# RWKV chunk products grouped by tile shape, and attention scores as 64-row products on both halves of the array

## The chip, the core and the metric

The kernel runs on one core of one Trainium2 chip. It is a single launch. The metric is device time in microseconds; lower is better. The core has a matrix engine (TensorE, PE in the profile, with its weight loads as PEld), a vector engine (VectorE, DVE), a scalar engine (ScalarE, ACT), GpSimd (POOL) and SyncE (SP), which issues all the transfers of this kernel from one queue. Products are written to PSUM, eight banks of 512 float32 columns on 128 partitions, and VectorE or ScalarE take them from there.

## What is computed

One step of a decoder layer for 512 prompt tokens and 8 x 4 sample tokens, 544 in all, with 1024 columns: a half-step feed-forward, a token-mixing sub-layer, a second half-step feed-forward, each with norms around it. The token mixing has two groups that work on the same projections: RWKV-7 with 8 heads of 64, and differential attention with 4 heads, each with two maps of 64 rows. Cut to what the change touches:

```python
def wkv_scan(r, w, k, v, kk, a, s0):
    def step(S, inp):
        r_t, w_t, k_t, v_t, kk_t, a_t = inp
        sa = jnp.einsum('bhvk,bhk->bhv', S, -kk_t)
        S = (S * w_t[:, :, None, :] + sa[..., None] * (kk_t * a_t)[:, :, None, :]
             + v_t[..., None] * k_t[:, :, None, :])
        return S, jnp.einsum('bhvk,bhk->bhv', S, r_t)
...
def diff_attend(q, k, v, q_pos, k_pos, table, lam):
    bias = rel_bias(q_pos, k_pos, table)
    s = jnp.einsum('bqhmd,bkhmd->bhmqk', q, k).astype(jnp.float32) * (A_QK_DIM ** -0.5)
    s = s + bias[None, :, None]
    s = jnp.where(k_pos[None, :] <= q_pos[:, None], s, NEG_INF)
    p = jax.nn.softmax(s, axis=-1)
    p = p[:, :, 0] - lam * p[:, :, 1]
    return jnp.einsum('bhqk,bkhd->bqhd', p.astype(v.dtype), v)
```

The kernel does the scan over the prompt in eight chunks of 64 tokens: within a chunk by products of its keys and queries, between chunks by a state of 64 x 64 for each head.

## The kernel before

**Layout.** Features lie on the partitions. Four tiles of 128 rows hold the eight RWKV heads, two to a tile: `b` counts the tiles, `e` the half (rows 0 to 63 or 64 to 127). An attention head is one tile of 128 rows, its two maps `m` again on the two halves. All products named here are float32, and the trace shows each such product as two records of weight load and of matmul. A product of 64 rows uses half the rows of the array, one with 64 output partitions half its columns; the profile writes the tile in front of the shape (`64*64 64x64` is a tile of 64 by 64 and a moving operand of 64 x 64).

**Stages.** Feed-forward (to about 420 us); projections of the RWKV columns with their preparation (to 584); inverses of the chunks' triangles on VectorE, beside the attention projections, with the first chunks in between (to 700); then attention over the prompt, the last chunks, the samples' RWKV chunk and the samples' attention over 32 pages of cache side by side (to about 823); output product; second feed-forward.

**A chunk.** `ahead(c)` does what needs only the chunk's own tokens: it loads `kbv` (keys, values) and `ar` (removal keys, queries) back from device memory, multiplies keys with both for each `b` and `e` (L755, tile 64 by 128, a bank for each `e`), masks them into `g` (L756), transposes (L759, L763) and forms the right-hand sides (L769). `chunk(c)` is the serial part: state against removal keys (L782), inverse (L788), next state (L795, tile 128 by 64), outputs: for each `b` and `e` state against queries (L806, tile 64 by 64) and behind it the chunk's own part (L807, tile 128 by 64), which adds to the same PSUM columns. Chunk 0 has no state product. Outputs are taken to `yr` by ScalarE (L808).

**Scores.** For each of 16 items (4 heads, 4 blocks of 128 queries, n = 128 to 512 keys) `scores` copies each map's 64 rows of the queries into its half of `qpad` (L904, ScalarE), whose other half is zero, and multiplies all 128 rows of it with all rows of the keys (L905). VectorE adds the bias and finds the maximum (L907), ScalarE exponentiates (L909). `weighted` transposes the result (L922) and multiplies it with the values (L927). Scores and `weighted` share three PSUM banks (`abank`); the last chunks' `ahead` has a single one (`xbank`).

**Order.** The order on each engine is not that of the source. The framework schedules all engines when the program is built, by its own times and by priorities (`advance` gives the serial part of a chunk high priority), and each engine then runs its list in that order. Transfers are issued by SP in the order of its list too, a transfer that must wait for a buffer holding back all behind it.

Of the kernel before, what the change touches and what calls it, by code (L numbers as in the profile page):

```python
# [9 lines left out]
FT = mybir.dt.float32  # L10
# [41 lines left out]
def build(ctx, tc, A):  # L52
# [38 lines left out]
    # matmuls ahead of the first data, so that the tensor engine's clock is up when it comes  # L91
# [15 lines left out]
    # ---------------------------------------------------------------- helpers  # L107
# [11 lines left out]
    def mm3(ps, w, x, first, last):  # L119
        """ps (+)= w.T @ x, each the exact sum of two float32r parts"""  # L120
        T.matmul(ps, w[0], x[0], start=first, stop=False)
        T.matmul(ps, w[0], x[1], start=False, stop=False)
        T.matmul(ps, w[1], x[0], start=False, stop=last)

    def dot(ps, w, xs, k0=0, ins=None):
        """ps = the sum over k of w[k].T @ xs[k], the parts of the weights that come last at the end"""
# [19 lines left out]
    def bank():  # L146
        return pw.tile([128, 512], FT, name="pb")
# [16 lines left out]
    def sums(pt, src, cols):  # L164
        """sums over the partitions that each of cols marks, of a half's tokens, which go on the partitions"""
# [4 lines left out]
    def sums4(ps, bank):  # L170
        """a half's sums, 32 rows (two times 16 alike) for each of four tiles, turned round: [token, tile, block, sum]"""
# [7 lines left out]
    def inv_sqrt(pt, n, scale=1.0, eps=None, least=None, y=None):  # L179
        """(scale * pt + eps) ** -0.5, or of at least `least`: a guess from the exponent, a step of  # L180
        the third order (two thirds of its result), a Newton step"""
# [23 lines left out]
    def spread(y, e, bank=bank):  # L205
        """tokens back to the free axis: each of a token's e values on its share of the partitions, in PSUM"""
# [30 lines left out]
    class Pre:  # L237
        """a block's input, gains applied; the rows' scale is left to whoever takes the product out"""
# [23 lines left out]
    def close_half(h, s, y, sq, gcol, pre=None, xp=None, spill=None, out=None):  # L262
        """the sub-layer's norm and residual, then the next one's input; in steps that other work goes between"""
# [44 lines left out]
    def opening(ws, xs, take):  # L308
        """the first products with a new input: half 1's side by side, as its rows get ready; taken out unscaled"""
# [14 lines left out]
    def products(wsrc, x, y, finish, per=1, wx=None, apart=False):  # L324
        """y[m] for all m and both halves, of weights that hold `per` m each; apart: half 1 after all of half 0"""
# [81 lines left out]
    # ---------------------------------------------------------------- first half-step  # L407
# [46 lines left out]
    # ---------------------------------------------------------------- token mixing  # L454
# [11 lines left out]
    # what lives from the projections to the output product  # L466
# [25 lines left out]
    def projected(i):  # L492
        """block i of the projected RWKV columns, behind the token before: what proj takes, what shifted reads"""
# [28 lines left out]
    def shifted(pr, dst, dsts):  # L522
        """mixed with the token before"""
# [55 lines left out]
    # negated biases over distances  # L579
# [10 lines left out]
    # a row for each partition, so that reading one place earlier on each gives a Toeplitz matrix  # L590
# [5 lines left out]
    for b in range(4):  # L596
# [14 lines left out]
        # decays: products over the chunk, of all tokens up to one and including it  # L611
# [6 lines left out]
        # removal keys, of unit length  # L618
# [11 lines left out]
        # keys and their share  # L630
# [45 lines left out]
    # unit triangular inverses: 32x32 blocks on one partition each, then one merge  # L676
# [25 lines left out]
    def merged():  # L702
        """the inverses' lower left blocks, in steps between the projections"""
# [27 lines left out]
    # queries, and in their place what they attend to  # L731
# [3 lines left out]
    # ---------------------------------------------------------------- RWKV, prompt: chunk after chunk  # L735
# [5 lines left out]
    def ahead(c, bank):  # L741
        """what a chunk needs from its own tokens alone"""
# [7 lines left out]
        kbt, vs = kv.rearrange("p (s b e k) -> p s b e k", s=2, b=4, e=2)[:, 0], kv.rearrange("p (s b e k) -> p s b e k", s=2, b=4, e=2)[:, 1]  # L750
        for e in range(2):
            rows = slice(e * HD, (e + 1) * HD)
            ps = bank()
            for b in range(4):
                T.matmul(ps[:, b * 128:(b + 1) * 128], kb[rows, b], ar[rows, b], start=True, stop=True)  # L755
            V.tensor_tensor(g[:, e], ps.rearrange("p (b t) -> p b t", t=128), gm, op=OP.mult)  # L756
# [8 lines left out]
        # right-hand sides: keys against values  # L765
# [9 lines left out]
    def chunk(c, state, ar, g, kbt, vs, rhs):  # L775
        # the state's part of the right-hand sides
# [14 lines left out]
        # next state  # L791
# [7 lines left out]
        # outputs  # L799
        ps = bank()  # L800
        for b in range(4):
            for e in range(2):
                rows = slice(e * HD, (e + 1) * HD)
                o = ps[rows, b * CH:(b + 1) * CH]
                if c:
                    T.matmul(o, state[rows, b], ar[rows, b, 1], start=True, stop=False)  # L806
                T.matmul(o, vs[:, b, e], g[:, e, b, CH:], start=not c, stop=True)  # L807
# [3 lines left out]
    # ---------------------------------------------------------------- attention projections  # L811
# [13 lines left out]
    def between(spot):  # L825
        """a step of the inverses' merging behind the products so far"""
# [44 lines left out]
    # ---------------------------------------------------------------- attention, prompt  # L871
    # lambda
# [11 lines left out]
    # negated biases: one Toeplitz tile for each head  # L884
# [7 lines left out]
    for t in qpads:  # L892
        G.memset(t, 0.0)
# [503 lines left out]
```

## Time and profile before

| | |
|---|---|
| median of 3 runs | 1316.78 us (1316.12, 1316.78, 1322.76) |
| span of the profiled execution | 1314.4 us |
| its time less the median | span 2.4 us below; no time beside the span is given for that execution |
| mean granted TensorE clock | 0.973 |
| PE busy | 1256.5 us (96%), 10354 matmul records |
| PEld busy | 1184.2 us (90%) |
| DVE / ACT / POOL busy | 696.4 / 461.2 / 503.1 us |
| L755, records and busy | 128, 16.6 us |
| L806 and L807, records and busy | 112, 18.4 us and 128, 19.4 us |
| L905, records in four widths, busy | 4 x 16, 2.5 + 5.0 + 5.9 + 7.5 us |

A record's duration is from its start to its modelled end, and records overlap, so mean durations do not add up to time on the path. What a group costs TensorE is read from the starts: that of its first record and that of the first record behind it. "Busy" of a group counts overlapping records once. The granted clock of a stretch is given beside its busy times, 1.00 for full speed.

### The profile page before, as it was taken

The page shows a single profiled execution, that of the slowest core. Times are in us where ns is not written, and L with a number is a line of the kernel's source. Part 1 is how long each engine was busy: PE and PEld are TensorE (multiplying, and loading weights), DVE is VectorE, ACT ScalarE, POOL GpSimd, SP SyncE. Part 2 cuts the span into 40 slices and gives each one's busy share as a digit, 9 for nine tenths or more (in the row PEclk, how much of TensorE's full clock was granted, in tenths as well). Part 3 has the DMA queues.
Part 4 walks back from the last instruction along what each step waited for, and adds up shares of the span by engine and source line. Part 5 has one row for each costly group of instructions (what it writes and reads, how often), then busy time and mean ns, then how long its engine had stood idle before and what let it go on. Part 6 is the DMA issues. An engine that isn't in the chain of part 4 may idle for free.

```text
span 1314.4 us, 25021 instructions
## 1 busy us (share of the span) xinstructions
PE 1256.5 (96%) x10354; PEld 1184.2 (90%) x10354; DVE 696.4 (53%) x1356; ACT 461.2 (35%) x878; POOL 503.1 (38%) x330
## 2 busy tenths in 40 slices
PE   8999999999998989989999999998899999999996
PEld 7999999999998888978887755888899999999995
DVE  7742034412448898879425367788842044412446
ACT  6433232312334444411114446555332233312331
POOL 2534433443346496633000022343534343433342
PEclk8999999999999999899899899999999999999998
DMA  5333223322232423353116357541323322322221
GB/s 198 99 95 97 81 81 97 95 83 81 85 109 87 150 87 124 135 180 110 59 50 190 129 177 262 182 131 47 113 81 97 94 79 86 97 85 79 82 61 68
DMA packets 54455, 142.06 MB, mean 108 GB/s; under 512 B 6050, under 2 KB 17058, under 8 KB 53191
## 3 DMA queue, kind: packets, MB, share of 16 engines
q1 hardware_dynamic: 54342, 140.48, 34.4%
q8 instruction: 81, 1.33, 0.4%
q14 instruction: 32, 0.25, 0.1%
HBM read 125.05 MB, written 16.72 MB: 108 GB/s over the span
## 4 chain that ended last, share of the span: by engine, by line
PE 45%; DVE 9%; ACT 1%; DMA 1%; issue 1%; SPq 0%; DVEq 0%; POOL 0%; ACTq 0%
PE mm L134 7%; PE mm L131 7%; PE mm L130 7%; PE pb L134 3%; PE pb L131 3%; PE pb L130 3%; DVE sqa L228 1%; PE pb L905 1%; DVE tmp L691 1%; PE pb L807 1%; PE pb L806 1%; PE pb L755 1%; DVE X L693 1%; PE pb L927 1%; PE mm L1099 1%
## 5 line engine op out<-in xcount | busy, mean ns | idle before, releaser
L116 POOL TENSOR_TENSOR wlo<-wraw,whi 128x1024 fp32r<-128x1024 f32 (+1 forms) x168 | 399.9, 2384 | 540.7 <-ACT whi L114 488.3
L130 PE MATMUL mm<-xh,whi 128*128 128x272 f32 x1160 | 303.1, 292 | 9.1 <-DVE q_f L820 3.5
L131 PE MATMUL mm<-xl,whi 128*128 128x272 f32 x1160 | 303.5, 293 | 4.7 <-DVE xl L248 4.7
L114 ACT ACTIVATE whi<-wraw 128x1024 fp32r<-128x1024 f32 (+1 forms) x176 | 182.6, 1039 | 253.8 <-PE mm L131 152.0
L130 PEld LDWEIGHTS mm<-xh,whi 128*128 128x128 f32 x1160 | 221.6, 191 | 11.3 <-DVE q_f L820 4.1
L131 PEld LDWEIGHTS mm<-xl,whi 128*128 128x128 f32 x1160 | 221.7, 191 | 6.6 <-DVE xl L248 6.3
L134 PE MATMUL mm<-xh,wlo 128*128 128x272 f32 x1160 | 179.4, 298 | 0.0
L134 PEld LDWEIGHTS mm<-xh,wlo 128*128 128x128 f32 x1160 | 162.8, 197 | 0.3
L130 PE MATMUL pb<-xh,whi 128*128 128x272 f32 x568 | 150.5, 295 | 1.6 <-ACT ga L371 0.9
L131 PE MATMUL pb<-xl,whi 128*128 128x272 f32 x568 | 149.2, 294 | 0.0
L358 DVE TENSOR_TENSOR up<-up,ga 128x272 f32<-128x272 f32 x88 | 111.7, 1271 | 8.2
L130 PEld LDWEIGHTS pb<-xh,whi 128*128 128x128 f32 x568 | 110.3, 194 | 2.8 <-ACT ga L371 1.1
L131 PEld LDWEIGHTS pb<-xl,whi 128*128 128x128 f32 x568 | 109.9, 194 | 0.3 <-issue 0.2
L387 DVE TENSOR_TENSOR up<-mm,rpre 128x272 f32<-128x272 f32 x54 | 23.8, 442 | 114.9 <-PE mm L134 114.8
L134 PE MATMUL pb<-xh,wlo 128*128 128x272 f32 x568 | 83.2, 288 | 0.0
L134 PEld LDWEIGHTS pb<-xh,wlo 128*128 128x128 f32 x568 | 75.6, 188 | 0.0
L357 ACT ACTIVATE ga<-ga 128x272 f32<-128x272 f32 x88 | 38.0, 432 | 71.5 <-DVE ga L386 63.4
L386 DVE TENSOR_TENSOR ga<-mm,rpre 128x272 f32<-128x272 f32 x53 | 23.2, 438 | 73.7 <-PE mm L134 73.7
L130 PE MATMUL mm<-hd0h,whi 128*128 128x272 f32 x242 | 62.0, 289 | 0.0
L131 PE MATMUL mm<-hd0l,whi 128*128 128x272 f32 x242 | 61.9, 288 | 0.0
L130 PE MATMUL mm<-hd1h,whi 128*128 128x272 f32 x220 | 56.4, 289 | 0.0
L131 PE MATMUL mm<-hd1l,whi 128*128 128x272 f32 x220 | 56.3, 288 | 0.0
(406 smaller groups left out, 2277.5 us busy)
## 6 DMA issues: line engine op xcount, KB each, us to landing
wraw<-in_ff_in_dram SPq DMA_DIRECT2D x87, 512.0 KB, 3.6
wraw<-in_ff_out_dram SPq DMA_DIRECT2D x32, 512.0 KB, 3.6
wraw<-in_w_in_dram SPq DMA_DIRECT2D x26, 512.0 KB, 3.9
pg<-in_cache_k_dram SPq DMA_DIRECT2D x32, 256.0 KB, 3.7
pg<-in_cache_v_dram SPq DMA_DIRECT2D x32, 256.0 KB, 5.1
wraw<-in_w_out_dram SPq DMA_DIRECT2D x16, 512.0 KB, 4.1
wraw<-in_ff_out_dram SPq DMA_DIRECT2D x16, 384.0 KB, 3.2
cat_d<-cat SPq DMA_DIRECT2D x4, 1280.0 KB, 5.0
```

Source lines behind the costliest of these rows:

```text
L114: S.activation(hi, raw, AF.Copy)
L116: eng.tensor_tensor(lo, raw, hi.bitcast(FT), op=OP.subtract)
L130: T.matmul(ps, hi, xs[k][0], start=k == 0, stop=False)
L131: T.matmul(ps, hi, xs[k][1], start=False, stop=False)
L134: latest[0] = T.matmul(ps, wcols(w, k0 + k)[1], xs[k][0], start=False, stop=k == n - 1).ins
L228: eng.tensor_tensor(self.acc, self.acc, sq, op=OP.add)
L357: S.activation(g, g, AF.Silu)
L358: V.tensor_tensor(u, u, g, op=OP.mult)
L386: V.tensor_tensor(g, pg, pre.rs[s], op=OP.mult)
L387: V.tensor_tensor(u, pu, pre.rs[s], op=OP.mult)
L691: V.tensor_tensor(tv, lb[:, j + 1:, j:j + 1].to_broadcast([128, n, m]), X[:, j:j + 1, :m].to_broadcast([128, n, m]), op=OP.mult)
L693: V.tensor_tensor(X[:, j + 1:, :m], X[:, j + 1:, :m], tv, op=OP.subtract)
```

## The change

Three edits; everything else is the same but for comments and docstrings, which are taken out, so that lines move by a few.

1. In `ahead`, both banks of L755 are taken first, and the products go `b` by `b`, with `e` as the inner loop; masking follows for both.
2. In `chunk`, the eight state products of the outputs come first, then the eight of the chunk's own part. As two halves of one bank are now open over four `b` at once, the first matmul of each half (`b == 0`) starts the accumulation and the last one ends it.
3. In `scores`, both maps' products come first, each of 64 rows of queries and keys, straight from `q_f` and `k_f`, on the half where they lie. `qpad`, its memsets and the copies of L904 go. Here the work on TensorE is named L898 after the change, the transposes L916, the product with the values L921; the outputs' own part is L808.

```diff
@@ ahead
-        for e in range(2):
-            rows = slice(e * HD, (e + 1) * HD)
-            ps = bank()
-            for b in range(4):
-                T.matmul(ps[:, b * 128:(b + 1) * 128], kb[rows, b], ar[rows, b], start=True, stop=True)
-            V.tensor_tensor(g[:, e], ps.rearrange("p (b t) -> p b t", t=128), gm, op=OP.mult)
+        pair = [bank() for _ in range(2)]
+        for b in range(4):
+            for e in range(2):
+                rows = slice(e * HD, (e + 1) * HD)
+                T.matmul(pair[e][:, b * 128:(b + 1) * 128], kb[rows, b], ar[rows, b], start=True, stop=True)
+        for e in range(2):
+            V.tensor_tensor(g[:, e], pair[e].rearrange("p (b t) -> p b t", t=128), gm, op=OP.mult)
@@ chunk
-        for b in range(4):
-            for e in range(2):
+        outs = [(b, e, ps[e * HD:(e + 1) * HD, b * CH:(b + 1) * CH]) for b in range(4) for e in range(2)]
+        if c:
+            for b, e, o in outs:
                 rows = slice(e * HD, (e + 1) * HD)
-                o = ps[rows, b * CH:(b + 1) * CH]
-                if c:
-                    T.matmul(o, state[rows, b], ar[rows, b, 1], start=True, stop=False)
-                T.matmul(o, vs[:, b, e], g[:, e, b, CH:], start=not c, stop=True)
+                T.matmul(o, state[rows, b], ar[rows, b, 1], start=b == 0, stop=False)
+        for b, e, o in outs:
+            T.matmul(o, vs[:, b, e], g[:, e, b, CH:], start=not c, stop=not c or b == 3)
@@ scores
-    # a head's two queries, each with zeros for the other's rows
-    qpads = [ap_.tile([128, 2, 128], FT, name=f"qpad{j}", bufs=1) for j in range(2)]
-    for t in qpads:
-        G.memset(t, 0.0)
...
-        qpads.append(qpads.pop(0))
-        qpad = qpads[-1]
...
+        both = [abank() for _ in range(2)]
         for m in range(2):
             rows = slice(m * 64, (m + 1) * 64)
-            ps = abank()
-            S.activation(qpad[rows, m], q_f[rows, i, qb * 128:(qb + 1) * 128], AF.Copy)
-            T.matmul(ps[:, :n], qpad[:, m], k_f[:, i, :n], start=True, stop=True)
+            T.matmul(both[m][:, :n], q_f[rows, i, qb * 128:(qb + 1) * 128], k_f[rows, i, :n], start=True, stop=True)
+        for m, ps in enumerate(both):
```

What the scheduler makes of it, at three places. On TensorE, around the outputs of one chunk (`set` holds `g` and the values, `x8` is eight instructions in a row), before:

```order
L795 MATMUL pb<-set 64x64
L905 MATMUL pb<-k_f,qpad_7710 128x256
L795 MATMUL pb<-set 64x64 x7
L806 MATMUL pb<-ar,state 64x64
L807 MATMUL pb<-set 64x64
...
L905 MATMUL pb<-k_f,qpad_7711 128x256 x2
```

and in the changed kernel:

```order
L898 MATMUL pb<-k_f,q_f 128x256
L796 MATMUL pb<-set 64x64 x8
L806 MATMUL pb<-ar,state 64x64 x8
L808 MATMUL pb<-set 64x64 x8
L898 MATMUL pb<-k_f,q_f 128x256 x3
```

The alternation of L806 and L807 is now two groups of eight, in every chunk from 1 to 7. The score products stand in pairs, of which two of the sixteen are separated by other work (the first of them here).

On TensorE, L755 of chunk 0, of chunk 3 and of the last chunk (the number of `pb` tells the bank, and so the half), in the changed kernel:

```order
L755 MATMUL pb_6434<-ar_6430,kbv_6428 128x128
L755 MATMUL pb_6435<-ar_6430,kbv_6428 128x128
L755 MATMUL pb_6434<-ar_6430,kbv_6428 128x128
...
L755 MATMUL pb_7288<-ar_7284,kbv_7282 128x128 x4
...
L755 MATMUL pb_7289<-ar_7284,kbv_7282 128x128 x4
...
L755 MATMUL pb_8351<-ar_8347,kbv_8345 128x128 x2
```

Chunk 0 alternates between the halves, and so does chunk 4 with other work in between; chunk 1 has three, three, one, one; chunks 2, 3, 5, 6 and 7 have all four of one half and then the other, as all had before. The two products of the last chunk now stand right behind the state product of chunk 6:

```order
L783 MATMUL pb<-state,ar 64x64 x8
L755 MATMUL pb<-ar,kbv 128x128 x2
L962 MATMUL mm<-cst,sx 128x128 x4
```

where before they came 32 rows of the order behind it, beyond the first page products. On SP, the transfers that they need, before:

```order
L1059 DMA tb_7888<-in_table_dram 32x4 x4
...
L1087 DMA pg_8238<-in_cache_k_dram 128x512
L744 DMA kbv<-cat_d 128x4x192
L746 DMA ar<-cat_d 128x4x128
```

and in the changed kernel (`pg` are pages of the cache, the `...` stands for sixteen of them):

```order
L1053 DMA tb_7878<-in_table_dram 32x4 x4
L746 DMA ar<-cat_d 128x4x128
...
L1081 DMA pg_8222<-in_cache_k_dram 128x512
L744 DMA kbv<-cat_d 128x4x192
```

`ar` of the last chunk moved ahead of the sixteen page loads, `kbv` stays behind them.

## The prediction

> **What bounds the kernel now.** I read the first part of the page, then the busy times in stretches of 20 us or so, then the order of time on TensorE. In the rows of stretches the first two columns are the stretch and its length, then the busy time of PE, PEld, DVE, ACT and POOL, the granted clock, the DMA share and GB/s.
>
> ```profile
> PE 1256.5 (96%) x10354; PEld 1184.2 (90%) x10354; DVE 696.4 (53%) x1356; ACT 461.2 (35%) x878; POOL 503.1 (38%) x330
> ...
> 700.00:720.00 20.00, 20.00 (x270) 15.26 (x268) 11.09 (x39) 11.57 (x32) 0.00 (x0) 1.00 0.77 218
> 760.00:780.00 20.00, 20.00 (x152) 9.40 (x151) 10.50 (x28) 7.69 (x24) 5.17 (x5) 1.00 0.63 185
> 780.00:800.00 20.00, 20.00 (x172) 11.87 (x171) 13.72 (x49) 11.63 (x33) 3.40 (x3) 1.00 0.88 304
> 800.00:825.00 25.00, 23.74 (x147) 13.35 (x146) 20.12 (x54) 15.96 (x36) 8.54 (x6) 1.00 0.67 226
> ```
>
> The change touches only what runs from 584 to 823 us. There TensorE is busy without a break up to 812 us, while VectorE and ScalarE have a third to a half of their time free. So what TensorE saves there comes off the end, until another engine is reached. Two waits say the same from the other side: VectorE and ScalarE stand waiting for exactly the products that the change edits (columns: total us, times, longest).
>
> ```profile
> DVE sc L907 <- PE pb L905: 15.5, 12, 4.1
> ...
> ACT yr L808 <- PE pb L807: 42.1, 8, 7.5
> ```
>
> **The outputs of a chunk.** Each product is two records. These are the first and the last rows of one chunk's output products, in order of time (start, length, what, tile, shape, records), and then two neighbours that stand in groups of one shape.
>
> ```profile
> 709.39 0.33 PE L806 MATMUL pb<-ar,state 64*64 64x64 f32 x2
> 709.64 0.33 PE L807 MATMUL pb<-set 128*64 128x64 f32 x2
> ...
> 713.24 0.33 PE L807 MATMUL pb<-set 128*64 128x64 f32 x2
> 713.50 1.13 PE L905 MATMUL pb<-k_f,qpad 128*128 128x256 f32 x4
> ...
> 715.68 0.68 PE L782 MATMUL pb<-state,ar 64*64 64x64 f32 x16
> 716.29 0.70 PE L905 MATMUL pb<-k_f,qpad 128*128 128x256 f32 x2
> ...
> 768.04 0.69 PE L795 MATMUL pb<-set 128*64 128x64 f32 x16
> 768.65 0.32 PE L806 MATMUL pb<-ar,state 64*64 64x64 f32 x2
> ```
>
> Start to start, the sixteen products take 713.50 - 709.39 = 4.11 us, 0.257 each. Eight products of the shape of L806 in one group take 716.29 - 715.68 = 0.61 us (L782, which also goes from half to half), and eight of the shape of L807 take 768.65 - 768.04 = 0.61 us (L795). Grouped, a chunk's outputs cost 1.22 us, and 2.89 us go. The order of the change shows the two groups whole in all seven chunks that have both kinds (chunk 0 has no state product): 7 x 2.89 = **20.2 us**. Whether the cost came from the change of shape, or from L807 adding onto the columns that L806 has only just written, does not matter here: both are removed.
>
> The Trainium skill, TensorEngine Tiling (Array Packing), section Restrictions and Gotchas, speaks against part of this: row tiles may not write one PSUM bank at the same time, and both halves' state products do go to one bank. By it the eight of L806 would run one after the other, some 0.4 us longer in each chunk, and the saving would be about 17 us, as an estimate from that section. L782 has the same layout and takes 0.61 us for eight, so the row decides.
>
> **The products of a chunk's own tokens (L755).** Eight products of 64 rows by 128 columns, four on one half and then four on the other.
>
> ```profile
> 584.46 1.68 PE L755 MATMUL pb<-ar,kbv 64*128 64x128 f32 x16 [0.34 <-DMA ar<-cat_d]
> 586.07 0.66 PE L759 MATMUL pb<-cst,kbv 128*128 128x128 f32 x4
> ```
>
> 1.61 us for eight, 0.20 each. Run in pairs they would save 0.8 us a chunk, 6.4 us in all. But the order built from the change alternates fully only for chunks 0 and 4 (there cut by other work) and in part for chunk 1; for the other five it still has one half after the other. Two to four pairs in each of three chunks, less the pair at the turn that already overlaps before: 1.1 us. Neighbours of another shape rise from 28 to 32; at 0.15 us a switch (the 0.257 of an output less the 0.10 that its 64 columns take at the rate of L755's 128) that costs 0.6. Net **0.5 us**.
>
> **The scores.** A pair of score products (both maps) now has 64 rows each, on the two halves. The row of the line with its four shapes (durations in ns, first and last start, shapes), and two pairs with the row behind each:
>
> ```profile
> L905 PE MATMUL pb<-k_f,qpad x64: 275/484/595, 705.6 to 812.3; 128*128 128x256 f32 x16, 128*128 128x128 f32 x16, 128*128 128x384 f32 x16, 128*128 128x512 f32 x16
> ...
> 781.48 1.46 PE L905 MATMUL pb<-k_f,qpad 128*128 128x384 f32 x4
> 782.86 0.68 PE L1182 MATMUL pb<-gsq,cst 128*32 128x272 f32 x2
> ...
> 788.95 1.88 PE L905 MATMUL pb<-k_f,qpad 128*128 128x512 f32 x4
> 790.77 1.91 PE L1099 MATMUL mm<-pg,qz 128*32 128x256 f32 x26
> ```
>
> Sixteen records of a shape are four pairs. A pair of 384 columns takes 1.38 us, one of 512 takes 1.82, so 128 columns of a pair cost 0.44 us and all sixteen pairs 4 x (1+2+3+4) x 0.43 = 17.1 us. That a product on each half runs at the same time is shown here only for tiles of 64 by 64 on the diagonal:
>
> ```profile
> 783.47 1.07 PE L1034 MATMUL mm<-vx,kvt 64*64 64x512 f32 x4
> 784.47 0.66 PE L1145 MATMUL mm<-cst,ov 128*128 128x128 f32 x4
> ```
>
> Two products of 512 columns in 1.00 us, where one alone of that width costs 0.85 (half of a pair above). For 64 by 128, where both halves write all 128 partitions, in two banks, no row shows it. Bounds: full overlap halves 17.1 and, with the two pairs that the order separates, saves 7.5; no overlap saves nothing. I take full overlap, since L1034 is the nearest row. Against it stand switches: neighbours of another shape go from 21 to 33, 12 x 0.10 to 0.15 = 1.2 to 1.8 us. Net **6.0 us** (from -1.8 to 6.3). The ScalarE copies of the queries go too, off the path: they cost ScalarE alone,
>
> ```profile
> L904 ACT ACTIVATE qpad<-q_f x32: 293/307/312, 690.6 to 797.9; 64x128 f32<-64x128 f32 x32
> ```
>
> 32 x 0.3 = 9.6 us where it is half idle. I cost them at nothing.
>
> **What is late next.** TensorE saves 20.2 + 0.5 + 6.0 = 26.7 us of work. Two things catch it. First the end of the stage, where the chain of waits already passes through VectorE (start, length, what):
>
> ```profile
> 812.95 0.69 DVE sc L907
> 813.99 0.92 DVE orp L1194
> 814.91 0.57 issue
> 815.48 0.50 DVE yr L1189
> ```
>
> VectorE is 80% busy from 800 us on, and 69% from 780. The scores that run behind 776 us (two pairs of 384 columns, four of 512) save 2 x 0.64 + 4 x 0.85 = 4.7 us, and most of that will be waited for: 3.5 (0 to 4.7). Second the keys of the last chunk. SP issues in its order:
>
> ```profile
> 696.08 18.03 SPq L1087 DMA_DIRECT2D pg<-in_cache_k_dram  x16
> 714.21 0.39 SPq L744 DMA_DIRECT2D kbv<-cat_d  x1
> ...
> L744 SPq DMA_DIRECT2D kbv<-cat_d x8: 359/374/497, 580.0 to 714.2; - x8
> DMA to landing us min/median/max: 3.3/3.5/4.9
> ...
> 730.11 1.12 PE L782 MATMUL pb<-state,ar 64*64 64x64 f32 x16
> 739.19 0.49 PE L755 MATMUL pb<-ar,kbv 64*128 64x128 f32 x2
> ```
>
> The load of kbv stays behind sixteen page loads, 18 us of issuing, and lands at 718 to 719 us. Before, L755 needs it at 739. In the changed order the first two of these products stand right behind the state product of chunk 6, which was at 730 (L782), and TensorE comes there five chunk outputs (14.5 us) and four score pairs of 256 columns (1.7 us) earlier: at 714. If SP's stream starts as early as before, everything on TensorE waits 5 us there; if it moves up with the projections that release it (two outputs stand ahead of them, 5.8 us), the load lands at 713 and nothing waits. I take 1.5 (0 to 5), and 1 for waits that I cannot name (0 to 3). Together **6 us given back** (0 to 13).
>
> **The clock.** Twice the clock falls just behind such output products (at 680 to 684 and 722 to 726 us):
>
> ```profile
> 680.00:684.00 4.00, 4.00 (x38) 2.96 (x34) 0.85 (x2) 0.00 (x0) 0.00 (x0) 1.00 0.00 0
> 684.00:688.00 4.00, 4.00 (x23) 3.65 (x23) 0.44 (x1) 0.38 (x1) 0.00 (x0) 0.57 0.25 69
> ...
> 724.00:728.00 4.00, 4.00 (x25) 3.12 (x24) 0.47 (x1) 0.77 (x2) 0.00 (x0) 0.68 0.00 0
> 728.00:732.00 4.00, 4.00 (x36) 2.35 (x35) 0.42 (x1) 1.31 (x8) 0.00 (x0) 0.50 0.01 4
> ```
>
> Lost: 4 x (0.43 + 0.32 + 0.50) = 5.0 us. If the alternation starved the array, both go; a new wait can bring one back (3.3). I take **2 us** gained (5.0 gained to 3.3 lost).
>
> **Sum.** -20.2 - 0.5 - 6.0 + 6 - 2 = -22.7 us against the span of 1314.4: 1291.7. The median of the runs shown is 1316.8, 2.4 above that span, so 1294.1.
>
> **Rivals.**
> 1. The halves of 64 by 128 do not overlap. For it: no row of such a pair. Against: L1034. The scores then only pay their switches (1.8) and L755 its 0.6; -20.2 + 2.4 + 4 (fewer waits) - 2 = -15.8, which gives 1301.
> 2. The gain is caught by waits: VectorE at the end and kbv in the middle at their full 13 us, with no gain of clock: -26.7 + 13 = -13.7, 1303; with a lost spell of clock as well, 1306. For it: the 80% of VectorE and the SP order. Against: SP's first load in that stream waits for TensorE, so it moves up too.
> 3. The full gain, waits near 1 and both spells of clock gone: -26.7 + 1 - 5 = -30.7, 1286.
> 4. Slower: arrays filled by halves and short waits keep the clock down in the whole stage from 640 to 800 us. From 45 us at half clock on, the 22.7 us are eaten; 60 us would give 1294 + 30 = 1324. For it: spells of 0.50 to 0.57 with TensorE busy by its records. Against: they follow the alternation that goes, and groups of halves (L782, L795) stand in stretches at 1.00. The Trainium skill, TensorE: Matmul & The Clock Gate, section Part 1: The HAM clock gate, tells of micro-idles between groups that make the gate oscillate; here only the two spells above look like it.
>
> That the change doesn't do what it says holds for L755, and stands in the sum.
>
> **Chances.** Forecast (1288 to 1299) 0.58; rival 1 0.14; rival 2 0.11; rival 3 0.12; rival 4 0.05. The range 1285 to 1306 takes in the forecast, rival 1, and most of 2 and 3, some 0.85. A measurement here tells about 0.5% (6.6 us) from nothing, so faster means below 1310.2: 0.92; within 0.5%: 0.04 (rival 2 at its worst); slower: 0.04.
>
> **What would show it.** Outputs: L806 and the line behind it in groups of 16 records, 0.61 us each. L755: alternate halves 0.1 us apart only in chunks 0, 1 and 4. Scores: a pair of 512 columns in 0.9 to 1.0 us rather than 1.82. Waits: TensorE idle for kbv or VectorE, 5 to 7 us between 640 and 810 us. Clock: 1.00 behind the outputs. Wrong if the outputs stay near 4 us, or if TensorE idles more than 13 us in that stage.

## The result and the profile after

The changed kernel takes 1289.65 us (median of four runs, 1288.69 to 1290.02), the kernel before on the same chip 1318.97 (median of four): ratio 0.9775, 95% interval 0.9753 to 0.9796. The profiled execution spans 1286.9 us where that of before spans 1314.4. The prediction was 1294 us (1285 to 1306) and faster. Intervals here and below leave out runs more than 1.5% above the fastest of their kernel; that left out three of the ten runs of the scores alone, at 1343 to 1346 us.

The page's first line of the changed kernel, and its rows by stretches (start and end of the stretch, its length, then the busy time of PE, PEld, DVE, ACT and POOL, the granted clock, the DMA share and GB/s):

```profile
PE 1225.1 (95%) x10354; PEld 1160.3 (90%) x10354; DVE 694.2 (54%) x1356; ACT 450.4 (35%) x846; POOL 501.9 (39%) x328
```

```profile
580.00:632.00 52.00, 45.27 (x468) 43.13 (x469) 48.70 (x91) 9.92 (x13) 18.37 (x8) 0.94 0.45 139
632.00:799.30 167.30, 162.78 (x1934) 115.64 (x1934) 91.85 (x278) 68.51 (x190) 18.88 (x19) 0.99 0.51 168
799.30:891.20 91.90, 85.83 (x649) 81.45 (x646) 80.77 (x164) 50.28 (x105) 35.09 (x23) 0.98 0.40 128
```

The second of these stretches ends with the first product of the output projection, the third with the first product of the last half-step. The same pieces of work of the kernel before, where these two products stand at 823.0 and 918.6 us:

```profile
580.00:632.00 52.00, 46.19 (x472) 44.15 (x472) 48.55 (x90) 9.75 (x12) 16.95 (x7) 0.95 0.45 136
632.00:823.00 191.00, 189.74 (x1931) 136.44 (x1925) 93.09 (x277) 78.67 (x219) 20.12 (x22) 0.96 0.47 148
823.00:918.60 95.60, 88.32 (x656) 82.46 (x653) 79.46 (x165) 51.29 (x109) 37.44 (x23) 0.98 0.38 122
```

This is the whole balance. The pieces are 338.6 us before and 311.2 after: 27.4 of the 27.5 us come from them. TensorE's busy time in them falls by 324.3 - 293.9 = 30.4 us, its idle time rises from 14.3 to 17.3, by 3.0. So almost all of TensorE's saving reached the end. (The prediction has TensorE busy without a break from 584 to 812 us. The rows show 5.8 us of idle time from 580 to 632 us, and 6.7 after the change; from 640 to 812 us the kernel before has none.)

The outputs of the chunk that the prediction showed at 709 us, now (start, length, line, tile, shape, records):

```profile
697.72 0.68 PE L806 MATMUL pb<-ar,state 64*64 64x64 f32 x16
698.34 0.69 PE L808 MATMUL pb<-set 128*64 128x64 f32 x16
698.95 0.91 PE L898 MATMUL pb<-k_f,q_f 64*128 64x256 f32 x5
```

698.95 - 697.72 = 1.23 us where it was 4.11. All seven chunks show 1.23. A pair of scores of 512 columns, and one of 384, each with the row behind it:

```profile
785.21 1.13 PE L898 MATMUL pb<-k_f,q_f 64*128 64x512 f32 x4
786.27 0.55 PE L214 MATMUL pb<-cst,rx 128*128 128x128 f32 x3
...
736.55 0.92 PE L898 MATMUL pb<-k_f,q_f 64*128 64x384 f32 x4
737.39 0.41 PE L1120 MATMUL mm<-cmb,ssc 128*32 128x128 f32 x2
```

1.06 us for 1.82, and 0.84 for 1.38: products of 64 by 128 on the two halves do overlap. Chunk 0's products of its own tokens alternate, and take 585.46 - 584.36 = 1.10 us for 1.61:

```profile
584.36 1.16 PE L755 MATMUL pb<-ar,kbv 64*128 64x128 f32 x16 [0.27 <-DMA ar<-cat_d]
585.46 0.66 PE L760 MATMUL pb<-cst,kbv 128*128 128x128 f32 x4
```

The new waits of TensorE are these (in brackets the idle time and what ended it):

```profile
711.99 0.68 PE L755 MATMUL pb<-ar,kbv 64*128 64x128 f32 x4 [1.01 <-DMA kbv<-cat_d]
...
789.50 0.55 PE L214 MATMUL pb<-cst,rx 128*128 128x128 f32 x3 [1.08 <-DVE yr L1183]
790.67 0.65 PE L1199 MATMUL mm<-fsq,ones 128*32 128x272 f32 x2 [0.62 <-ACT fsq L1198]
...
794.88 0.68 PE L1176 MATMUL pb<-gsq,cst 128*32 128x272 f32 x2 [1.12 <-ACT gsq L1175]
```

And the clock, in the stretches where the kernel before had 0.57, 0.68 and 0.50:

```profile
684.00:688.00 4.00, 4.00 (x76) 3.41 (x75) 2.43 (x12) 0.68 (x2) 0.00 (x0) 1.00 0.70 214
724.00:728.00 4.00, 4.00 (x74) 2.62 (x74) 2.74 (x12) 1.87 (x7) 0.00 (x0) 1.00 0.39 122
728.00:732.00 4.00, 3.78 (x43) 3.00 (x41) 2.74 (x16) 3.01 (x10) 0.00 (x0) 1.00 0.91 292
```

### The profile page after: what moved, and what is told of

It reads as the page before. It is cut to its first block, busy times and chain, and to the rows that moved or that the text cites. A ratio compares the mean times of both kernels' runs of the same rounds, so it can differ in the third digit from the quotient of the medians.

```text
span 1286.9 us, 24967 instructions
## 1 busy us (share of the span) xinstructions
PE 1225.1 (95%) x10354; PEld 1160.3 (90%) x10354; DVE 694.2 (54%) x1356; ACT 450.4 (35%) x846; POOL 501.9 (39%) x328
## 4 chain that ended last, share of the span: by engine, by line
PE 75%; DVE 18%; DMA 2%; ACT 2%; issue 2%; POOL 0%; SPq 0%; DVEq 0%; ACTq 0%
PE mm L134 14%; PE mm L131 14%; PE mm L130 14%; PE pb L131 7%; PE pb L130 7%; PE pb L134 7%; DVE sqa L228 2%; DVE xl L248 2%; DVE tmp L691 2%; DVE pn L276 1%; PE pb L755 1%; DVE X L693 1%; PE mm L1093 1%; PE pb L898 1%; PE pb L168 1%
## 5 line engine op out<-in xcount | busy, mean ns | idle before, releaser
L130 PE MATMUL mm<-xh,whi 128*128 128x272 f32 x1160 | 304.2, 293 | 10.2 <-DVE ga L386 2.7
L134 PE MATMUL mm<-xh,wlo 128*128 128x272 f32 x1160 | 176.3, 295 | 0.0
L358 DVE TENSOR_TENSOR up<-up,ga 128x272 f32<-128x272 f32 x88 | 114.9, 1308 | 8.2
L228 DVE TENSOR_TENSOR sqa<-sqa,sq 128x272 f32<-128x272 f32 x73 | 56.1, 776 | 17.6 <-ACT sq L227 16.4
```

The costliest lines, as they stand in the source:

```text
L130: T.matmul(ps, hi, xs[k][0], start=k == 0, stop=False)
L134: latest[0] = T.matmul(ps, wcols(w, k0 + k)[1], xs[k][0], start=False, stop=k == n - 1).ins
L228: eng.tensor_tensor(self.acc, self.acc, sq, op=OP.add)
L358: V.tensor_tensor(u, u, g, op=OP.mult)
```

## The experiments

### One edit at a time

Three kernels, each the kernel before with one of the three edits.

```diff
 e1: the outputs in two groups (each edit abridged)
+for b, e, o in outs:
+    T.matmul(o, state[rows, b], ar[rows, b, 1], start=b == 0, stop=False)
+for b, e, o in outs:
+    T.matmul(o, vs[:, b, e], g[:, e, b, CH:], start=not c, stop=not c or b == 3)
 e2: scores of 64 rows
-T.matmul(ps[:, :n], qpad[:, m], k_f[:, i, :n], start=True, stop=True)
+T.matmul(both[m][:, :n], q_f[rows, i, qb * 128:(qb + 1) * 128], k_f[rows, i, :n], start=True, stop=True)
 e3: L755 half by half in turn, into two banks
+pair = [bank() for _ in range(2)]
+for b in range(4):
+    for e in range(2):
+        T.matmul(pair[e][:, b * 128:(b + 1) * 128], kb[rows, b], ar[rows, b], start=True, stop=True)
```

> Kernel before with the second edit alone: a chunk's state outputs in one group, then its own-part outputs in one group; L755 and the scores stay as before. Theory (the gain is the alternation of shapes in the outputs, and the two half-clock spells belong to it): 7 x 2.89 = 20.2 us of TensorE work go, both spells between 680 and 732 us go (5 us, of which some 0.5 lies inside the outputs' own figure), 1 to 2 us come back as waits, so 22 to 25 us less than before, ratio 0.981 to 0.983. Rival a (the spells come from the scores or from L755): -18 to -20 us with a granted clock of 0.5 to 0.7 still in two stretches of 4 us between 640 and 800 us. Rival b (the outputs' gain was caught by waits and the scores made the rest): under 15 us.

> Kernel before with the third edit alone: score products of 64 rows on both halves, no padded queries. Theory: a pair of 512 columns goes from 1.82 to 1.06 us as in the changed kernel, all pairs save 6 us, 1 to 3 of them are waited for at the end of the stage where VectorE is 80% busy, so 3 to 6 us less than before; the outputs stay at 4.1 us a chunk and at least one half-clock spell stays. Rival (the scores hide waits that the outputs would otherwise meet, or the spells go with the padded queries): 8 us or more less, with clock 1.00 from 640 to 800 us.

> Kernel before with the first edit alone: the products of a chunk's own tokens written half by half in turn into two banks. Theory: only chunks 0 and 4 and part of 1 come out alternating, net 0.5 us, so within 2 us of before. Rival (the order of the other work changes with it, through the two banks that are taken at once): 2 to 6 us either way.

Measured against 1319.6 us of the kernel before on that chip (its runs from 1315.4 to 1327.2): the outputs alone 1296.5 us, ratio 0.981 (0.977 to 0.985), as expected. The scores alone are not faster but **slower**, 1328.6 us, ratio 1.010 (1.006 to 1.015), and the pairs alone too, 1334.7 us, 1.012 (1.007 to 1.016). By these ratios the first part saves 25 us and the other two lose 13 and 15 (by the medians 23, 9 and 15); together the three save 29. That was in no expectation.

The outputs alone show the two groups in all seven chunks, 705.45 - 704.23 = 1.22 us here, beside the old scores:

```profile
704.23 0.68 PE L805 MATMUL pb<-ar,state 64*64 64x64 f32 x16
704.84 0.69 PE L807 MATMUL pb<-set 128*64 128x64 f32 x16
705.45 1.13 PE L905 MATMUL pb<-k_f,qpad 128*128 128x256 f32 x4
```

No half clock stands behind them. There is a new spell of it, though, from 645 to 652 us, before the first of these groups; it comes up again at the end.

In the trace of the scores alone their line did what it should, 13.36 us for 19.16. L755 in the pairs alone did not: it takes 17.58 us for 15.60, with 24 of its 128 records at half clock. What grew is, first of all, time at half clock. These are stretches of the pairs-only kernel, cut where its clock changes:

```profile
681.57:684.98 3.41, 3.41 (x27) 2.54 (x27) 0.08 (x1) 0.11 (x1) 0.00 (x0) 1.00 0.00 0
684.98:688.39 3.41, 3.41 (x17) 3.16 (x18) 0.00 (x0) 0.28 (x1) 0.00 (x0) 0.50 0.33 82
695.22:698.63 3.41, 3.41 (x28) 2.53 (x28) 1.52 (x9) 0.00 (x0) 0.00 (x0) 1.00 0.65 221
698.63:708.87 10.24, 10.24 (x67) 8.25 (x67) 3.09 (x8) 2.32 (x5) 0.00 (x0) 0.50 0.71 204
...
746.42:749.83 3.41, 3.41 (x28) 2.54 (x28) 1.20 (x5) 0.00 (x0) 0.00 (x0) 1.00 0.00 0
749.83:753.25 3.42, 3.42 (x18) 1.52 (x18) 0.00 (x0) 0.77 (x2) 0.00 (x0) 0.50 0.04 10
```

And of the kernel before, cut in the same way:

```profile
681.04:684.45 3.41, 3.41 (x27) 2.54 (x28) 0.14 (x1) 0.05 (x1) 0.00 (x0) 1.00 0.00 0
684.45:687.87 3.42, 3.42 (x15) 3.18 (x15) 0.44 (x1) 0.34 (x1) 0.00 (x0) 0.50 0.29 80
722.00:725.41 3.41, 3.41 (x34) 2.54 (x30) 2.13 (x8) 1.15 (x5) 0.00 (x0) 1.00 0.00 0
725.41:732.24 6.83, 6.83 (x49) 4.64 (x49) 0.42 (x1) 2.08 (x10) 0.00 (x0) 0.50 0.01 2
```

Two things are to be seen. First, the clock changes only on a grid of 3.413 us: from 684.45 to 725.41 are 40.96 us, twelve steps; in the other kernel from 684.98 to 698.63 are 13.65, four steps, and to 749.83 are 64.85, nineteen. From the start of the span the grid lies elsewhere in every execution. Second, the window of the grid ahead of each of these half-clock stretches is full of alternating outputs: in the kernel before 3.26 us of the one that starts at 681.04 (chunk 2's outputs run from 680.2 to 684.3), 3.22 of that at 722.00. Over the traces of the kernel before, of the scores alone and of the pairs alone, the full-clock windows that hold 3.08 us or more of these products are eleven, and all eleven are followed by half clock. Of the windows at full clock that hold some of them, but less (up to 2.97 us, the one at 769.8 in the kernel before), none is. TensorE is busy without a break in all of them: 3.41 of 3.41 us.

The Trainium skill, TensorE: Matmul & The Clock Gate, section Part 1: The HAM clock gate, gives a free-running window of 3413 ns. The traces agree to the last digit that they show. It calls the windows that lower the clock idle; these eleven are not idle by the records, and the measurement decides: it is not only recorded idle time that lowers the clock. (The ends of the records are modelled, so gaps that they hide are not ruled out.)

So a chunk's stretch of 4.11 us is longer than a window, and whether it fills one hangs on where the grid happens to lie. The kernel before had three half-clock windows behind its outputs, the scores alone five (and one more behind a wait of 1.9 us at 815), the pairs alone nine. Six more windows at half clock are 6 x 3.41 / 2 = 10.2 us of the 18.0 by which the profiled execution of the pairs alone is longer. Over its whole span it has 94.4 us at half clock for 70.2, worth 12.1 us, and TensorE idles 63.7 us for 57.9: together 17.9. The scores alone have 74.8 us at half clock in all, worth 2.3 us, and idle 6.9 us more (64.8), against the 5.8 that their line saves: 3.4 of the 5.4 us by which their profiled execution is longer, and the other 2 stay open. (That is the fastest of their runs; the mean clock of the others is 0.964 or less, that of this one 0.972.) The runs of the kernel before lie 12 us apart, with mean clocks from 0.976 down to 0.966. A share of 0.010 of 1320 us is 13 us, so the clock accounts for the spread; that the place of the grid makes it is argued, since these runs have no traces.

### What an alternating output costs: shape or columns

The prediction left open whether the 0.257 us of an alternating product came from the change of shape or from adding onto columns just written. Two orders of the same sixteen products in the changed kernel, S for a state output and V for an own-part output:

```diff
 e4 (11 changes of shape, V two products behind its S)
+for k, (b, e, o) in enumerate(outs):
+    T.matmul(o, state..., ar...)            # S(k)
+    if k >= 2: own(*outs[k - 2])            # V(k - 2)
 e5 (7 changes of shape)
+for b in range(4):
+    S(b, 0); S(b, 1); V(b, 0); V(b, 1)
```

> The changed kernel with the sixteen outputs of a chunk in another order: each own-part product comes two products behind the state product whose columns it adds to, with another state product between, so the shape still changes 11 times within a chunk (15 before, 1 in the changed kernel) but no product adds onto columns that the product just ahead of it wrote. Theory (the change of shape costs): by changes, 1.22 + 10 x (4.11 - 1.22) / 14 = 3.3 us a chunk, so 7 x 2.1 = 14 us slower than the changed kernel, and up to 5 more if the half-clock spells come back. Rival (adding onto columns just written costs): 1.2 to 1.5 us a chunk, within 2 us of the changed kernel.

> The changed kernel with the outputs of each block as two state products, then two own-part products: 7 changes of shape within a chunk, where the kernel before has 15, the skewed order 11 and the changed kernel 1. Theory (each change of shape costs about 0.206 us, whatever columns are added to): 1.23 + 6 x 0.206 = 2.47 us a chunk, 7 x 1.24 = 8.7 us slower than the changed kernel, so 1297 to 1300 us. Theory of the clock (a stretch of alternating outputs of 3.0 us or more within one of the clock's windows of 3.41 us halves the clock after it): 2.47 us never fills a window, so no half-clock spell behind outputs. Rival (the cost sits in the alternation of single products, pairs of one shape escape it): below 1.7 us a chunk.

Measured: 1308.1 us (ratio 0.990, 0.987 to 0.994) and 1296.3 us (0.982, 0.979 to 0.985). One chunk of the first, from its first output to the row behind the last (691 - 694 us), and part of one of the second:

```profile
690.87 0.44 PE L807 MATMUL pb<-ar,state 64*64 64x64 f32 x6
691.24 0.33 PE L803 MATMUL pb<-set 128*64 128x64 f32 x2
691.50 0.33 PE L807 MATMUL pb<-ar,state 64*64 64x64 f32 x2
...
693.80 0.45 PE L803 MATMUL pb<-set 128*64 128x64 f32 x6
694.18 0.44 PE L847 MATMUL pb<-cst,vf 128*128 128x128 f32 x2
```

```profile
700.76 0.33 PE L810 MATMUL pb<-ar,state 64*64 64x64 f32 x4
701.02 0.34 PE L808 MATMUL pb<-set 128*64 128x64 f32 x4
...
702.60 0.34 PE L808 MATMUL pb<-set 128*64 128x64 f32 x4
702.87 1.13 PE L900 MATMUL pb<-k_f,q_f 64*128 64x256 f32 x6
```

694.18 - 690.87 = 3.31 us a chunk, the 3.3 of the theory of shapes; the theory of columns, with 1.2 to 1.5, falls. (The profiled execution of this kernel is 14.0 us longer than the changed kernel's, as expected; its median is 18 longer.) The second is 702.87 - 700.76 = 2.11, below the 2.47 expected: a pair of one shape costs 0.26 us, as much as one product alone did. So two things are lost by alternation, which I had taken for one. The two prices are fitted: from 1.23 us (2 groups) and 2.11 (8 groups), with the halves overlapping in both, a change of shape costs (2.11 - 1.23) / 6 = 0.147 us and a pair of products 0.117; a single product between others costs that 0.117 too, for it has no partner. The other two orders test the fit: by it the kernel before comes to 16 x 0.264 = 4.2 (measured 4.11) and the skewed order, with 12 groups and 14 pairs or single products, to 3.4 (3.31). Of the 2.89 us saved in a chunk some 2.0 are changes of shape and 0.9 are halves that run side by side again.

Neither kernel has half clock behind its outputs in its profile: 2.11 us cannot fill a window to 3.08, and 3.31 can for (3.31 - 3.08) + (3.41 - 3.08) = 0.56 of 3.41 us of phases, one stretch in six by this estimate. The runs of the skewed order, from 1302.3 us to 1316.8 with mean clocks from 0.978 to 0.964, fit that; only one near the fast end has a trace.

### The alternation kept, but cut in two

If full windows lower the clock, the alternation may stay as long as no window is full. The kernel before, with the next state's eight products between two halves of the outputs, and the scores' edit alone on top of that:

```diff
 e6 (on the kernel before), e7 (the same with the scores' edit)
 for b in range(4):
     S(b, 0); V(b, 0); S(b, 1); V(b, 1)
+    if b == 1:
+        the eight products of the next state
```

> Kernel before with the same sixteen outputs of a chunk in the same alternating order, but cut in two by the eight products of the next state, which before stood ahead of them. TensorE has the same products with as many changes of shape; only no window of 3.41 us can hold 3.0 us of alternation any more (2.06 + 0.74 = 2.80 at most). Theory of the clock: the granted clock is 1.00 behind every output, the 4 to 10 us that the spells cost before go, and the times of the runs lie closer together than those of before (1315 to 1327). Rival (the spells belong to the amount of alternation, or to other work): spells as before and a time within 2 us of before.

> The scores' edit alone, on the kernel with the cut outputs. Theory (the scores' edit is worth 6 us of TensorE, and alone on the kernel before it came out 9 us slower only since its new places on the windows' grid turned more output stretches into half-clock spells): 3 to 6 us faster than the cut kernel without it, clock 1.00 behind the outputs. Rival (the edit itself lowers the clock or brings waits that eat it): the same time as the cut kernel without it, or slower.

Measured beside 1321.2 us of the kernel before (1315.7 to 1328.0): 1312.2 us cut (ratio 0.9925, 0.990 to 0.995; 1309.2 to 1315.0) and 1311.8 with the scores (0.9945, 0.992 to 0.997). The cut kernel's clock from 639 us, the end of the spell that all these kernels have there, to the end of the stage:

```profile
639.14:720.00 80.86, 80.86 (x1038) 68.63 (x1038) 30.89 (x90) 24.50 (x64) 3.03 (x8) 1.00 0.35 106
720.00:823.00 103.00, 101.33 (x907) 61.50 (x906) 62.72 (x201) 54.55 (x160) 16.90 (x14) 1.00 0.62 206
```

No half-clock window is left in this execution, with the second half of the alternation still at 2.05 us, and the runs lie half as far apart as before. The 9 us are not the clock's alone, though: the first product of a chunk's outputs came out apart from the rest and the next state has a neighbour of its own shape, so that outputs and next state together take 32.6 us for 36.4.

The scores on the cut kernel met the rival. Their line takes 13.05 us for 19.02, but the median moved by 0.4 us, and the span of the profiled executions by 2.5. Its new waits on TensorE, 3.1 us more up to the last product of the attention, are mostly at the group norms, where VectorE and ScalarE set the pace.

### What the scores are worth in the changed kernel

The changed kernel again, and the changed kernel without the scores' edit, on one chip:

> The changed kernel itself once more, so that the others of this call are compared with it on one chip: 1288.5 to 1291 us, since no stretch of its outputs can fill a window of the clock, against 1315 to 1328 for the kernel before, whose time hangs on how many output stretches fall into such windows.

> The changed kernel with the scores' edit undone (128-row products of padded queries), the other two edits kept. Theory (the scores are worth 6 us of TensorE, of which 2 to 4 are waited for again where the group norms meet VectorE): 2 to 6 us slower than the changed kernel. Rival (on the cut outputs the edit was worth nothing, so here too all of it is caught by waits): within 1 us of the changed kernel.

1291.7 us (ratio 0.977, 0.974 to 0.979; one run as low as 1288.6) and 1293.6 (0.978, 0.976 to 0.980); the profiled executions 1286.8 and 1291.1. The runs of the two overlap, so by time alone the 2 us between the medians are not certain; and of the 4.3 us between the profiled executions only 1.8 lie in the stage that the edit touches (214.4 and 216.2 us from the first L755 to the output projection). So the edit is worth some 2 us here, at the lower end of what was expected. The changed kernel itself came out above its 1288.5 to 1291 us, and its five runs lie 6 us apart (1288.6 to 1294.9). Without the edit the scores' line takes 18.94 us for 13.07, 5.9 more, and TensorE idles 1.9 us instead of 4.4 up to the last product of the attention: 2.5 of the 5.9 come back as waits, and 1.0 in L921's products, which cost 11.28 us behind the new scores and 10.24 behind the old ones.

### Further along the same way

Two kernels that go on from the changed one: the state outputs moved up behind L783, which has their shape, and then L755's two banks taken from two pools, so that the halves alternate in more chunks.

```diff
 e8 / e8b
 T.matmul(ps..., ar[rows, b, 0], state[rows, b])     # L783, eight
+po = bank()
+T.matmul(po..., state[rows, b], ar[rows, b, 1])     # state outputs, eight
 ...
 T.matmul(ps..., kbt[:, b, e], vs[:, b, e])          # next state, eight
 T.matmul(po..., vs[:, b, e], g[:, e, b, CH:])       # own part, eight
 e9, on top of e8
-pair = [bank() for _ in range(2)]
+pair = [abank(), xbank()] if c < 6 else [xbank(), mbank()]
```

> The changed kernel with the group of state outputs moved up behind the state's part of the right-hand sides, which has its shape, into a bank of its own; the own-part outputs then stand behind the next state, which has theirs. Two changes of shape less in each of seven chunks: theory of the shapes 14 x 0.15 to 0.21 = 2 to 3 us faster than the changed kernel, 1286 to 1288 us. Rival (the bank held from there on delays the inverses or the next state): 1 to 4 us slower than the changed kernel, with TensorE idle ahead of those.

> The state outputs moved behind the products of their own shape, once more beside the changed kernel: the theory of 0.147 us a change of shape gives 14 x 0.147 = 2.1 us less than the changed kernel, the first look gave 2.5. Rival (a difference between chips): the same time as the changed kernel within 1 us.

> The early state outputs, and the products of a chunk's own tokens in two banks of different pools, so that the halves alternate in chunks 0 to 3 and 5, where so far they do in 0, 4 and part of 1. Theory (eight products cost 1.10 us where the halves alternate and 1.61 where they do not): up to 3 x 0.5 = 1.5 us less than without it. Rival (the bank is taken from the products that it also serves, and TensorE waits for it): 1 to 5 us more.

The early state outputs: 1287.1 us on one chip (ratio 0.975, 0.973 to 0.978), and on another, beside the changed kernel, 1288.6 (1286.7 to 1294.0) where that has 1291.7 (1288.6 to 1294.9). The runs of the two overlap, so by time alone the 3 us are not certain. The traces have them: L783, the inverses, the next state and both outputs take 22.7 us for 24.9, 2.2 less where 14 x 0.147 = 2.1 were due, and the spans are 1284.9 and 1286.8. By its medians it is the fastest kernel here.

The pairs in two pools lost: 1297.7 us (0.981, 0.979 to 0.983), 9 us more than without them and beyond the 1 to 5 of the rival. L755 did save what it should, 13.0 us for 14.65. But the last chunk's load of kbv, which the prediction named, was waited for longer, 2.71 us for the 1.01 of the changed kernel,

```profile
718.85 1.13 PE L755 MATMUL pb<-ar,kbv 64*128 64x128 f32 x8 [2.71 <-DMA kbv<-cat_d]
```

and half-clock windows stand at 700, 721 and 799 us again, with no alternating outputs ahead of them; in all five runs the mean clock is 0.970. In the windows ahead of the three, TensorE is busy for 2.91, 1.79 and 1.57 of 3.41 us. The second holds the wait for kbv, so this wait was followed by a loss of clock as well:

```profile
717.23:720.64 3.41, 1.79 (x19) 1.53 (x21) 0.62 (x2) 0.14 (x2) 0.00 (x0) 1.00 0.22 71
720.64:724.06 3.42, 3.42 (x39) 2.88 (x33) 1.72 (x7) 1.07 (x6) 0.00 (x0) 0.50 0.00 0
```

Not all of the loss is there: at 571 us, ahead of the first L755, TensorE waits 5.75 us for VectorE, for 1.28 us in the kernel without the pools.

## Why the prediction was right, and where it was off

Its sum was -22.7 us of span, measured were -27.5. Term by term, start to start on TensorE from 580 us to the first product of the last half-step:

| term | predicted | measured |
|---|---|---|
| outputs of the chunks | -20.2 | -20.65 (29.90 to 9.25 us) |
| L755 | -0.5 | -0.4 (15.60 to 15.23) |
| scores | -6.0 | -6.1 (19.16 to 13.07) |
| waits given back | +6 | +4.2 (3.0 idle, 1.2 in L921 and L789) |
| clock | -2 | -4.7 (the remainder: all other lines together) |

**The three edits** were sized right, each to half a microsecond, by the rows they were taken from: L782 and L795 for a group of eight, L1034 for halves that overlap. So rival 1 falls (1.06 us for the pair of 512 columns). The scores' 6 us hold some luck, for both sides of the difference were 2 us too low: their line costs 19.16 us before, where 17.1 was taken, and 13.07 after, where 17.1 - 6.0 = 11.1 was. A pair of 512 columns takes a little more than half, 1.06 us and not the 0.9 to 1.0 named as the sign. That both halves' state products write one bank cost nothing: eight of L806 take 0.61 us, as L782's did. So the rule that the prediction weighed against that row (the Trainium skill, TensorEngine Tiling (Array Packing), section Restrictions and Gotchas) does not show here; for the 0.4 us a chunk that the prediction put to it, no run shows a source. The order did keep L755's alternation in chunks 0, 4 and part of 1 alone.

**One sentence failed**, though the sum did not hang on it: "Whether the cost came from the change of shape, or from L807 adding onto columns ... does not matter here". It is the change of shape, and beside it the lost overlap of the halves. Had I split the 0.257 us so, the move of the early state outputs, 2 us more, would have been on the page before the result.

**The waits** were named right and sized somewhat high (TensorE idles 4.5 us from 632 to 799 us, where 5 to 7 were the sign): kbv at 1.01 us for the 1.5 taken, and 2.8 us at the group norms for the 3.5 of VectorE's end. The row that ends the 1.08 us is VectorE's; the other two are ScalarE's squares, and the last of them stands behind a step of ScalarE that waited 0.89 us for GpSimd. So the group norms hold TensorE up, as forecast, but not through VectorE alone.

**The clock** is the term that was mis-sized: 2 us taken from a range of 5.0 to -3.3, where 4.7 are left over and the three half-clock windows behind the outputs, worth 5.1 us, are all gone. The prediction saw that the falls "follow the alternation", but set against them a new wait that could bring one back. No such wait came here, though the pairs in two pools show one. The runs show a rule: in these traces every full-clock window of 3.41 us filled to 3.08 or more with alternating outputs was followed by half clock, and a stretch of 1.23 us can fill none. An estimate from these numbers: a stretch of 4.11 us fills a window to 3.08 for (4.11 - 3.08) + (3.41 - 3.08) = 1.36 of each 3.41 us of phases, four times in ten; with seven chunks that is 2.8 windows in an execution, and at 1.7 us for each half-clock window 4.8 us that the edit takes away on average, more where the half clock lasts for several windows. Rival 3 (full gain, waits near 1, both spells gone) had the clock right and the waits too low; rival 2's 13 us of waits came to 4.2, and rival 4's half clock from 640 to 800 us is absent from the changed kernel. What rival 4 feared, a kernel made slower through its clock, did happen on the kernel before, with two of the three edits alone. But there the half clock stood behind the alternating outputs, which those kernels keep, and once behind a wait, not behind arrays filled by halves.

## What to carry to other kernels

Group TensorE's products by tile shape, and let products on the two halves alternate inside a group: here (float32, 64 columns) a change of shape costs 0.147 us, and a product without a partner on the other half costs 0.117, as much as a pair, whatever columns they write. When a part of a change looks harmful alone, look at the granted clock in windows before judging it: an edit that only shifts the work can move badly filled stretches onto the clock's grid, and what it saves itself is then not seen. A stretch of poorly filled products that must stay can be cut by others so that no 3.4 us are full of it. A new wait can cost twice: its own length, and half clock behind it.

## What was not expected of the hardware

The clock fell with TensorE busy in every nanosecond of the records, eleven times of eleven behind windows with 3.08 us or more of alternating products, on a grid of 3.413 us whose place differs from one execution to the next. That other products do the same is seen, but not settled: in the outputs-only kernel the window from 641.8 us holds none of these products, but small ones of four shapes (32 by 32, 64 by 64, 64 by 128 and 128 by 128), and half clock follows:

```profile
641.80:645.20 3.40, 3.40 (x48) 2.91 (x48) 1.25 (x3) 0.74 (x2) 0.00 (x0) 1.00 0.02 5
645.20:652.00 6.80, 6.80 (x66) 6.41 (x66) 3.01 (x5) 0.60 (x1) 0.00 (x0) 0.50 0.00 0
```

Half clock stands behind waits too. The spell from about 626 to 637 us, which both kernels have and which costs each of them some 5 us by the same estimate, begins behind a window in which TensorE is busy for 0.74 of 3.41 us (0.40 in the changed kernel), waiting for VectorE. So it does not come from the 32 by 32 products of L709, which start only at 626.5 us, inside it:

```profile
623.01:626.42 3.41, 0.74 (x6) 0.52 (x5) 3.41 (x3) 0.00 (x0) 1.96 (x1) 1.00 0.01 2
626.42:636.66 10.24, 9.32 (x152) 8.69 (x153) 5.96 (x11) 1.07 (x2) 0.00 (x0) 0.50 0.36 120
```

Busy time alone does not decide, however: in the changed kernel windows with 2.33 and 2.29 us busy (from 786.4 and 793.3 us) were not followed by half clock, and the one with 2.91 us in the kernel with two pools was. What the gate counts, where its threshold lies for a mix of shapes, and why the spell at 626 us lasts for three windows, stays open.
